# Rotary embedding on one core: half-size loads on two queues, earlier late loads, two more rows added by TensorE

## Chip, cores and metric

One core of a Trainium2 chip runs the kernel. The metric is the device time of one execution in microseconds (us); smaller is better. The time of a kernel is the median of its runs. "Profile" means one further execution, taken by the hardware profiler, whose span runs from the first instruction of the kernel to the last; its trace also has a record of every packet that the core's 16 DMA engines moved (queue, start, length, bytes).

## What is computed

`x` is 16 x 512 x 1024 in float32, 8192 vectors of 16 heads with 64 numbers each; `cos` and `sin` are 512 x 32. Each head is rotated:

```
x = x.reshape(batch, seq, num_heads, head_dim)
x1, x2 = x[..., :half_dim], x[..., half_dim:]
cos, sin = cos[None, :, None, :], sin[None, :, None, :]
rotated = concatenate([x1 * cos - x2 * sin, x1 * sin + x2 * cos], axis=-1)
```

So 33.5 MB are read and 33.5 MB written, with two multiplications and one addition for each number.

## The kernel before

**Tiles and rows.** The 8192 vectors are cut into eight tiles of 1024 (`TILES`, L33). A tile lies as 8 vectors on each of 128 partitions, and the kernel works by "rows": row `u` = 0 to 63 is one vector on each partition, 128 x 1024 numbers, and tile `t` has rows 8t to 8t + 7. A tile of 8 rows is 4 MB, with 32 KB on each partition. `x_sb` is a ring with places for 40 rows, five tiles; the sixth, seventh and eighth tile take the places of the first, second and third, and results are written over the input in the ring before they are stored.

**An entry of `TILES`** has the number of rows, the place in the ring, the pieces it is loaded in, the pieces it is stored in, and (last) the numbers of the stores that must have landed before it is loaded. Loads and stores are numbered in order of tiles. Before, the first tile is loaded as two halves (loads 0 and 1), all others whole (loads 2 to 8). The stores are 0 and 1 (halves of the first tile), 2 to 7 (whole tiles), 8 and 9 (halves of the last).

**Who does what for a row.** VectorE multiplies the row with the cosines (`mul`, L341) into one of three PSUM places (`NT1`). GpSimd multiplies the row, with its halves swapped, with the signed sines into one of six SBUF places `t2_sb` (`NT2`), for two rows at once (L308) or one (L165); VectorE does that itself for one row of each tile and a few more of the first (`V2`). The two products are added either by VectorE (`comb`, L350), or, where `PE2[u]` is set (L68), by TensorE, which multiplies `t2_sb` with the identity onto the PSUM place in four pieces of the row's two PSUM banks (L268), after which ScalarE copies the sum to `x_sb` (L230). Before, TensorE has rows 5 and 7 and, from row 8 to row 51, the second, fourth and sixth row of each tile. VectorE's order is written out: `mul(u)`, then `comb(u - 1)` where TensorE has not taken it (L357 to L365).

**The queues.** ScalarE's queue (`on_scalar`, L206) issues all loads of `x`: the six of the first five tiles at the very start, the other three ("late") behind a row of its copies (`BEHIND`, L45), after a wait for the stores that free their place. SyncE's queue (`on_sync`, L194) issues the two small tables of sines and cosines, and then every store, each as soon as its last row has been added. A queue hands its DMAs on in the order in which it issues them. The page calls ScalarE's queue q10 and SyncE's q1. Both feed the same 16 DMA engines, and each DMA of `x` is 8 packets on every engine: a packet is one partition's part, 32 KB for a whole tile, 16 KB for a half.

**Waiting for a load.** `wait_landed` (L190) makes GpSimd and VectorE wait at the first row of each load.

Of the kernel before, what the change touches and what calls it, by code (L numbers as in the profile page):

```python
# [6 lines left out]
def bass_split_heads_rope_kernel(  # L7
# [14 lines left out]
    R1 = seq // P  # L22
# [6 lines left out]
    COPY = mybir.ActivationFunctionType.Copy  # L29

    TILES = (  # L33
        (8, 0, (4, 4), (4, 4), ()),
        (8, 8, (8,), (8,), ()),
        (8, 16, (8,), (8,), ()),
        (8, 24, (8,), (8,), ()),
        (8, 32, (8,), (8,), ()),
        (8, 0, (8,), (8,), (0, 1)),
        (8, 8, (8,), (8,), (2,)),  # L40
        (8, 16, (8,), (4, 4), (3,)),
    )
    RING = 40

    BEHIND = {6: 21, 7: 28, 8: 37}  # L45
    first_row = [sum(t[0] for t in TILES[:i]) for i in range(len(TILES))]
    NU = sum(t[0] for t in TILES)
    assert NU * P == batch * seq
    NT = len(TILES)
# [2 lines left out]

    loads = []
    stores = []
    for t, (n, place, ins, outs, _) in enumerate(TILES):
        assert sum(ins) == n == sum(outs) and place + n <= RING
        loads += [(t, sum(ins[:i]), m) for i, m in enumerate(ins)]
        stores += [(t, sum(outs[:i]), m) for i, m in enumerate(outs)]
    load_at = {(t, o): i for i, (t, o, _) in enumerate(loads)}
    store_after = {first_row[t] + o + m - 1: i for i, (t, o, m) in enumerate(stores)}  # L60
    late = [i for i, (t, _, _) in enumerate(loads) if TILES[t][4]]
    awaited = sorted({k for t in TILES for k in t[4]})


    V_ROWS = {8: (3, 6)}
    V2 = [r in V_ROWS[TILES[t][0]] and (t == 0 or r != 6) for t, r in rows]

    PE2 = [u in (5, 7) or R1 * 2 <= u < NU - 3 * R1 and u % 8 in (1, 3, 5) for u in range(NU)]  # L68

    def count(flags):  # L70
        return [sum(flags[: u + 1]) for u in range(NU)]
# [5 lines left out]
    CUT = 5 * H // 8  # L77
    n_pe = count(PE2)
    n_comb = count([not a for a in PE2])

# [10 lines left out]
    with ExitStack() as stack:  # L91
# [13 lines left out]
        sem_in = [stack.enter_context(nc.semaphore(f"in{i}")) for i in range(len(loads))]  # L105
        sem_out = {k: stack.enter_context(nc.semaphore(f"out{k}")) for k in awaited}
# [24 lines left out]
        for n in SIZES:  # L131
            m = len(V_ROWS[n]) * HD
# [10 lines left out]
        xf = x.rearrange("b s d -> (b s) d")  # L143
        of = out.rearrange("b s h d -> (b s) (h d)")

        def in_dram(flat, t, o, m):
            n = TILES[t][0]
            run = flat[first_row[t] * P:(first_row[t] + n) * P, :].rearrange("(p r) d -> p (r d)", r=n)
            return run[:, o * dim:(o + m) * dim]

        def place_of(u):
            t, r = rows[u]
            return TILES[t][1] + r

        def in_sbuf(t, o, m):
            k = TILES[t][1] + o
            return x_sb[:, k:k + m].rearrange("p n h t d -> p (n h t d)")
# [14 lines left out]
        def wait_added(eng, u):  # L172
            if n_pe[u]:
                eng.wait_ge(sem_a, n_pe[u])
            if n_comb[u]:
                eng.wait_ge(sem_v, n_comb[u])

        def wait_t2_free(eng, u):
            if u >= NT2:
                v = u - NT2  # L180
                if PE2[v]:
                    eng.wait_ge(sem_e, n_pe[v])
                else:
                    eng.wait_ge(sem_v, n_comb[v])

        def load(eng, i):
            t, o, m = loads[i]
            eng.dma_start(in_sbuf(t, o, m), in_dram(xf, t, o, m)).then_inc(sem_in[i], 16)

        def wait_landed(eng, t, r):  # L190
            if (t, r) in load_at:
                eng.wait_ge(sem_in[load_at[t, r]], 16)

        def on_sync(sp):  # L194
            for c, table, sem in ((1, sin, sem_sin), (0, cos, sem_cos)):
                sp.dma_start(stage[:, c, :], table.rearrange("(s r) d -> s (r d)", r=R1)).then_inc(sem, 16)  # L196
            for u in range(NU):
                if u not in store_after:
                    continue
                k = store_after[u]  # L200
                t, o, m = stores[k]
                wait_added(sp, u)
                sp.dma_start(in_dram(of, t, o, m), in_sbuf(t, o, m)).then_inc(sem_out.get(k, sem_rest), 16)
            sp.wait_ge(sem_rest, 16 * (len(stores) - len(awaited)))

        def on_scalar(ae):  # L206
            early = [i for i in range(len(loads)) if i not in late]
            for i in early:
                load(ae, i)
            ae.wait_ge(sem_i, 2)  # L210
            for n in SIZES:
                m = n // R1
                ae.activation(  # L213
                    pick[n][:],
                    ident[:].rearrange("q (s k) -> q k s", k=m)[:, :, None, :].broadcast_to([P, m, m, P // m]),
                    COPY,
                ).then_inc(sem_g, 1)
            for i, n in enumerate(SIZES):
                ae.wait_ge(sem_t, i + 1)
                ae.activation(s_sb[n][:, :, 0, :], raw_sin[n], COPY, scale=-1.0)  # L220
                ae.activation(s_sb[n][:, :, 1, :], raw_sin[n], COPY).then_inc(sem_s, 1)  # L221
            for n in SIZES:
                v = V_ROWS[n]
                some = raw_sin[n][:, v[0]:v[-1] + 1:max(1, v[-1] - v[0]), :]
                ae.activation(v_ps[n][:, :, 0, :], some, COPY, scale=-1.0)
                ae.activation(v_ps[n][:, :, 1, :], some, COPY).then_inc(sem_s, 1)
            for u in range(NU):
                if PE2[u]:
                    ae.wait_ge(sem_e, n_pe[u])
                    ae.activation(xs[:, place_of(u), :], t1_ps[:, u % NT1, :], COPY).then_inc(sem_a, 1)  # L230
                for i in late:
                    if BEHIND[i] == u:
                        for j in TILES[loads[i][0]][4]:
                            ae.wait_ge(sem_out[j], 16)
                        load(ae, i)

        def on_tensor(pe):
            pe.wait_ge(sem_z, 1)
            for k in range(NT1):
                for b in range(EH):  # L240
                    pe.matmul(  # L241
                        t1_ps[:, k, b * BANK:(b + 1) * BANK], zero[:, 0:P], zero[:], start=True, stop=True
                    ).then_inc(sem_w, 1)
            pe.wait_ge(sem_g, len(SIZES))
            pe.wait_ge(sem_cos, 16)
            pe.wait_ge(sem_sin, 16)
            pe.wait_ge(sem_w, NT1 * EH)
            for n in SIZES:
                for c, to in enumerate((c_ps[n], raw_sin[n])):
                    for k in range(n // R1):  # L250
                        ins = pe.matmul(  # L251
                            to[:, k * R1:(k + 1) * R1, :].rearrange("p r d -> p (r d)"),
                            pick[n][:, k].rearrange("q b s -> q (b s)"),
                            stage[:, c, :],
                            start=c == 0,
                            stop=True,
                            skip_group_check=c == 1,
                        )
                ins.then_inc(sem_t, 1)
            for u in range(NU):  # L260
                if not PE2[u]:
                    continue
                if TWO[u - 1]:
                    pe.wait_ge(sem_q[(u - 1) % NT2], made[u - 1])
                pe.wait_ge(sem_q[u % NT2], made[u])
                t2 = t2_sb[:, u % NT2, :, :, :].rearrange("p h t d -> p (h t d)")
                for b in range(EH):
                    ins = pe.matmul(  # L268
                        t1_ps[:, u % NT1, b * BANK:(b + 1) * BANK],
                        ident[:],  # L270
                        t2[:, b * BANK:(b + 1) * BANK],
                        start=False,
                        stop=True,
                        skip_group_check=True,
                    )
                ins.then_inc(sem_e, 1)

        def on_gpsimd(pl):
# [12 lines left out]
            for u in range(NU):  # L291
# [9 lines left out]
                for v in range(u, u + m):  # L301
                    if v == u + m - 1 or PE2[v - NT2] != PE2[v + 1 - NT2]:
                        wait_t2_free(pl, v)
# [13 lines left out]
        def on_vector(ve):  # L317
# [39 lines left out]
            for u in range(NU + LEAD):  # L357
# [6 lines left out]
                if u >= LEAD and not ahead and not PE2[u - LEAD]:  # L364
                    comb(u - LEAD)  # L365

        on_sync(nc.sync)
        on_scalar(nc.scalar)
        on_gpsimd(nc.gpsimd)
        on_tensor(nc.tensor)  # L370
        on_vector(nc.vector)

# [32 lines left out]
```

## Time and profile before

| what | value |
|---|---|
| time, median of 3 runs | 161.31 us (161.09 to 161.41) |
| time of the profiled execution | 160.98 us |
| its span | 159.7 us |
| VectorE busy | 133.8 us (84%), 119 instructions |
| GpSimd busy | 126.3 us (79%), 40 instructions |
| TensorE busy | 60.5 us (38%), 90 matmuls |
| ScalarE busy | 22.1 us (14%), 25 instructions |
| moved by DMA | 67.25 MB, mean 421 GB/s over the span |
| ScalarE's queue, SyncE's queue | 49.4% and 49.1% of the time of 16 engines |

"Busy" is the sum of an engine's instructions. The page also cuts the span in 40 slices of 4 us and gives for each the busy share of every engine and of the DMA engines, as digits in tenths. "Landing" is the moment at which a DMA's completion has been counted by all 16 engines; until then no one may use its data.

### The profile page before, as it was taken

What the parts mean: (1) busy time and instruction counts of PE and PEld (TensorE: products, weight loads), DVE (VectorE), ACT (ScalarE), POOL (GpSimd) and SP (SyncE); (2) the same over time, 40 slices, a digit from 0 to 9 for tenths busy, and PEclk for the clock granted to TensorE, in tenths of its full rate; (3) what the DMA queues carried; (4) which work ended last, traced back from release to release, by engine and by line L of the source; (5) the groups of instructions that cost most, each with busy time, mean ns of one, the idle gap of its engine ahead of it and who ended that gap; (6) DMA issues with size and microseconds to landing.
All of it is one profiled execution on the core that took longest, in us unless ns stands there. A gap on an engine that the chain in (4) does not pass through costs nothing.

```text
span 159.7 us, 449 instructions
## 1 busy us (share of the span) xinstructions
PE 60.5 (38%) x90; PEld 20.9 (13%) x90; DVE 133.8 (84%) x119; ACT 22.1 (14%) x25; POOL 126.3 (79%) x40
## 2 busy tenths in 40 slices
PE   6013001893540954089509870854098100000000
PEld 1013001130110221023102220211022000000000
DVE  0005897999999999999899989999999899999600
ACT  0302000114220042011500250052002200000000
POOL 1003999999999999999999999999999699940000
PEclk9999999999996599755995576599755955555555
DMA  5999999999998999999999999999999999999896
GB/s 176 440 410 451 443 476 394 394 460 394 394 509 369 501 394 394 501 412 402 451 460 402 418 492 394 402 484 427 402 443 468 394 427 484 402 402 484 373 447 271
DMA packets 3025, 67.25 MB, mean 421 GB/s; under 512 B 336, under 2 KB 592, under 8 KB 592
## 3 DMA queue, kind: packets, MB, share of 16 engines
q10 hardware_dynamic: 1296, 33.56, 49.4%
q1 hardware_dynamic: 1728, 33.69, 49.1%
q14 instruction: 1, 0.01, 0.0%
HBM read 33.69 MB, written 33.55 MB: 421 GB/s over the span
## 4 chain that ended last, share of the span: by engine, by line
DVE 63%; PE 11%; POOL 8%; DMA 6%; ACT 3%; issue 2%; SPq 0%; POOLq 0%
DVE t_ps L341 35%; DVE x_sb L350 23%; PE t_ps L268 9%; DMA stage<-in_cos_dram 6%; DVE t_sb L165 6%; POOL t_sb L165 5%; POOL t_sb L308 3%; ACT x_sb L230 3%; PE tab_ps L251 1%; PE t_ps L251 1%; ACT sine L220 0%; SPq L196 0%; ACT sine L221 0%; POOLq L299 0%
## 5 line engine op out<-in xcount | busy, mean ns | idle before, releaser
L308 POOL TENSOR_TENSOR t_sb<-x_sb,sine 128x2048 f32<-128x2048 f32 x22 | 99.1, 4526 | 1.6 <-DMA x_sb<-in_x_dram 1.3
L341 DVE TENSOR_TENSOR t_ps<-x_sb,tab_ps 128x1024 f32<-128x1024 f32 x64 | 76.8, 1221 | 14.1 <-PE t_ps L251 12.5
L268 PE MATMUL t_ps<-t_sb,ident 128*128 128x512 f32 x76 | 55.7, 881 | 55.1 <-DVE t_ps L341 41.2
L350 DVE TENSOR_TENSOR x_sb<-t_ps,t_sb 128x1024 f32<-128x1024 f32 x45 | 54.5, 1215 | 1.6 <-POOL t_sb L308 0.9
L165 POOL TENSOR_TENSOR t_sb<-x_sb,sine 128x1024 f32<-128x1024 f32 (+1 forms) x12 | 27.3, 2288 | 13.0 <-ACT sine L221 13.0
L230 ACT ACTIVATE x_sb<-t_ps 128x1024 f32<-128x1024 f32 x19 | 19.5, 1024 | 91.5 <-PE t_ps L268 91.5
L268 PEld LDWEIGHTS t_ps<-t_sb,ident 128*128 128x128 f32 x76 | 18.4, 269 | 91.1 <-issue 59.6
L165 DVE TENSOR_TENSOR t_sb<-x_sb,tab_ps 128x1024 f32<-128x1024 f32 (+1 forms) x9 | 10.2, 1135 | 0.0
L251 PE MATMUL tab_ps<-stage,chosen 128*128 128x128 f32 x4 | 1.2, 454 | 7.5 <-DMA stage<-in_cos_dram 7.5
L241 PE MATMUL t_ps<-zero 128*128 128x512 bf16 x6 | 2.7, 627 | 1.2 <-DVE zero L318 1.2
L251 PEld LDWEIGHTS tab_ps<-stage,chosen 128*128 128x128 f32 x4 | 0.9, 322 | 8.4 <-issue 8.4
L213 ACT ACT_TABLE_LOAD x1 | 1.3, 1283 | 3.8 <-issue 3.8
L220 ACT ACTIVATE sine<-t_ps 128x256 f32<-128x256 f32 x1 | 0.4, 384 | 8.1 <-PE t_ps L251 8.1
L251 PE MATMUL t_ps<-stage,chosen 128*128 128x128 f32 x4 | 1.1, 421 | 0.0
L318 DVE MEMSET zero<- 128x256 uint32 x1 | 0.3, 272 | 0.9 <-PEq L387 0.9
L241 PEld LDWEIGHTS t_ps<-zero 128*128 128x128 bf16 x6 | 0.7, 135 | 2.4 <-DVE zero L318 1.2
L251 PEld LDWEIGHTS t_ps<-stage,chosen 128*128 128x128 f32 x4 | 1.0, 333 | 0.0
L279 POOL MEMSET ident<- 128x128 f32 x1 | 0.2, 205 | 0.3 <-POOLq L387 0.3
L213 ACT ACTIVATE chosen<-ident 128x256 f32<-128x256 f32 x1 | 0.4, 430 | 0.0
L221 ACT ACTIVATE sine<-t_ps 128x256 f32<-128x256 f32 x1 | 0.4, 377 | 0.0
L281 POOL TENSOR_SCALAR_AFFINE_SELECT ident<-ident 128x128 f32<-128x128 f32 x1 | 0.3, 293 | 0.1
L387 POOL MEMSET const-float32-0.0<- 128x1 f32 x1 | 0.1, 98 | 0.3 <-issue 0.3
(5 smaller groups left out, 0.7 us busy)
## 6 DMA issues: line engine op xcount, KB each, us to landing
x_sb<-in_x_dram ACTq DMA_DIRECT2D x7, 4096.0 KB, 29.1
out_dram<-x_sb SPq DMA_DIRECT2D x6, 4096.0 KB, 28.5
out_dram<-x_sb SPq DMA_DIRECT2D x4, 2048.0 KB, 15.4
x_sb<-in_x_dram ACTq DMA_DIRECT2D x2, 2048.0 KB, 9.7
stage<-in_sin_dram SPq DMA_DIRECT2D x1, 64.0 KB, 5.5
stage<-in_cos_dram SPq DMA_DIRECT2D x1, 64.0 KB, 10.2
```

The source lines that it names most:

```text
L165: return eng.tensor_tensor(t2_sb[:, u % NT2, a:b, :, :], swapped(place_of(u))[:, a:b], table[:, None, :, :].broadcast_to([P, b - a, 2, HALF]),
L213: ae.activation(pick[n][:], ident[:].rearrange("q (s k) -> q k s", k=m)[:, :, None, :].broadcast_to([P, m, m, P // m]), COPY,).then_inc(se ...
L220: ae.activation(s_sb[n][:, :, 0, :], raw_sin[n], COPY, scale=-1.0)
L221: ae.activation(s_sb[n][:, :, 1, :], raw_sin[n], COPY).then_inc(sem_s, 1)
L230: ae.activation(xs[:, place_of(u), :], t1_ps[:, u % NT1, :], COPY).then_inc(sem_a, 1)
L241: pe.matmul(t1_ps[:, k, b * BANK:(b + 1) * BANK], zero[:, 0:P], zero[:], start=True, stop=True).then_inc(sem_w, 1)
L251: ins = pe.matmul(to[:, k * R1:(k + 1) * R1, :].rearrange("p r d -> p (r d)"), pick[n][:, k].rearrange("q b s -> q (b s)"), stage[:, c, :] ...
L268: ins = pe.matmul(t1_ps[:, u % NT1, b * BANK:(b + 1) * BANK], ident[:], t2[:, b * BANK:(b + 1) * BANK], start=False, stop=True, skip_group ...
L281: pl.affine_select(out=ident[:], in_=ident[:], compare_op=mybir.AluOpType.is_equal, fill=0.0, base=0, pattern=[[-1, P]], channel_multiplier=1,
L308: pl.tensor_tensor(t2_sb[:, u % NT2:u % NT2 + 2].rearrange("p n h t d -> p (n h) t d"), x_sb[:, k:k + 2, :, ::-1, :].rearrange("p n h t d ...
L341: ve.tensor_tensor(t1_ps[:, u % NT1, :].rearrange("p (h d) -> p h d", d=HALF), x_sb[:, k, :, :, :].rearrange("p h t d -> p (h t) d"), c_ps ...
L350: ve.tensor_tensor(xs[:, place_of(u), :], t1_ps[:, u % NT1, :], t2_sb[:, u % NT2, :, :, :].rearrange("p h t d -> p (h t d)"), add,).then_i ...
```

## The change

- The second and third tile are loaded as two halves each. The first halves (loads 2 and 4) stay on ScalarE's queue; the second halves (loads 3 and 5) are issued by SyncE, behind the two tables and before all stores.
- The sixth tile is loaded as two halves too. With that the loads are numbered 0 to 11, and the late ones are 8 and 9 (halves of the sixth tile), 10 and 11 (the seventh and the eighth). They are issued behind rows 13, 21, 29 and 37, after a wait for store 0, 1, 2 and 3. Before, the three late loads stood behind rows 21, 28 and 37, the first of them after stores 0 and 1.
- Both halves of a tile other than the first count on one semaphore, and the tile's first row waits for both.
- `PE2` goes on to row 57: TensorE adds rows 53 and 57 as well.
- TensorE waits for the first load before it makes the tables.

```
     TILES = (
-        (8, 0, (4, 4), (4, 4), ()),
-        (8, 8, (8,), (8,), ()),
-        (8, 16, (8,), (8,), ()),
-        (8, 24, (8,), (8,), ()),
-        (8, 32, (8,), (8,), ()),
-        (8, 0, (8,), (8,), (0, 1)),
-        (8, 8, (8,), (8,), (2,)),
-        (8, 16, (8,), (4, 4), (3,)),
+        (8, 0, (4, 4), (4, 4)),
+        (8, 8, (4, 4), (8,)),
+        (8, 16, (4, 4), (8,)),
+        (8, 24, (8,), (8,)),
+        (8, 32, (8,), (8,)),
+        (8, 0, (4, 4), (8,)),
+        (8, 8, (8,), (8,)),
+        (8, 16, (8,), (4, 4)),
     )
...
-    BEHIND = {6: 21, 7: 28, 8: 37}
+    FREED_BY = {8: 0, 9: 1, 10: 2, 11: 3}
+    BEHIND = {8: 13, 9: 21, 10: 29, 11: 37}
+    ON_SYNC = (3, 5)
...
-    PE2 = [u in (5, 7) or R1 * 2 <= u < NU - 3 * R1 and u % 8 in (1, 3, 5) for u in range(NU)]
+    PE2 = [u in (5, 7) or R1 * 2 <= u < NU - 6 and u % 8 in (1, 3, 5) for u in range(NU)]
...
         def wait_landed(eng, t, r):
-            if (t, r) in load_at:
-                eng.wait_ge(sem_in[load_at[t, r]], 16)
+            if t == 0 and r == loads[1][1]:
+                eng.wait_ge(sem_in[1], 16)
+            if t > 0 and r == 0:
+                eng.wait_ge(sem_in[first_load[t]], 16 * len(TILES[t][2]))

         def on_sync(sp):
             for c, table, sem in ((1, sin, sem_sin), (0, cos, sem_cos)):
                 sp.dma_start(stage[:, c, :], table.rearrange("(s r) d -> s (r d)", r=R1)).then_inc(sem, 16)
+            for i in ON_SYNC:
+                load(sp, i)
...
-            early = [i for i in range(len(loads)) if i not in late]
+            early = [i for i in range(len(loads)) if i not in late and i not in ON_SYNC]
...
                 for i in late:
                     if BEHIND[i] == u:
-                        for j in TILES[loads[i][0]][4]:
-                            ae.wait_ge(sem_out[j], 16)
+                        ae.wait_ge(sem_out[FREED_BY[i]], 16)
                         load(ae, i)
...
             pe.wait_ge(sem_w, NT1 * EH)
+            pe.wait_ge(sem_in[0], 16)
```

More of the change, by code (lines that the diff above doesn't have):

```diff
@@ L54, in bass_split_heads_rope_kernel @@
     stores = []
-    for t, (n, place, ins, outs, _) in enumerate(TILES):
+    for t, (n, place, ins, outs) in enumerate(TILES):
         assert sum(ins) == n == sum(outs) and place + n <= RING
@@ L58, in bass_split_heads_rope_kernel @@
         stores += [(t, sum(outs[:i]), m) for i, m in enumerate(outs)]
-    load_at = {(t, o): i for i, (t, o, _) in enumerate(loads)}
     store_after = {first_row[t] + o + m - 1: i for i, (t, o, m) in enumerate(stores)}
-    late = [i for i, (t, _, _) in enumerate(loads) if TILES[t][4]]
-    awaited = sorted({k for t in TILES for k in t[4]})
+    first_load = [[v for v, _, _ in loads].index(t) for t in range(NT)]
+    late = sorted(FREED_BY)
+    awaited = sorted(FREED_BY.values())
     V_ROWS = {8: (3, 6)}
     V2 = [r in V_ROWS[TILES[t][0]] and (t == 0 or r != 6) for t, r in rows]
-    PE2 = [u in (5, 7) or R1 * 2 <= u < NU - 3 * R1 and u % 8 in (1, 3, 5) for u in range(NU)]
+    PE2 = [u in (5, 7) or R1 * 2 <= u < NU - 6 and u % 8 in (1, 3, 5) for u in range(NU)]
     def count(flags):
@@ L187, in load @@
             t, o, m = loads[i]
-            eng.dma_start(in_sbuf(t, o, m), in_dram(xf, t, o, m)).then_inc(sem_in[i], 16)
+            eng.dma_start(in_sbuf(t, o, m), in_dram(xf, t, o, m)).then_inc(sem_in[first_load[t] if t else i], 16)
         def wait_landed(eng, t, r):
-            if (t, r) in load_at:
-                eng.wait_ge(sem_in[load_at[t, r]], 16)
+            if t == 0 and r == loads[1][1]:
+                eng.wait_ge(sem_in[1], 16)
+            if t > 0 and r == 0:
+                eng.wait_ge(sem_in[first_load[t]], 16 * len(TILES[t][2]))
         def on_sync(sp):
```

## The prediction

> **What bounds the kernel now.** I read the page's slices and queues first, then the waits of SyncE's queue, then the end of the chain, then GpSimd's timeline and the DMA issues around the last load.
>
> ```profile
> DMA  5999999999998999999999999999999999999896
> ...
> q10 hardware_dynamic: 1296, 33.56, 49.4%
> q1 hardware_dynamic: 1728, 33.69, 49.1%
> ```
>
> The DMA engines are the bound: after the first slice they are busy to the end, and the two queues' packets take 98.5% of the span. In the trace's packet records, all 16 engines have a packet in flight from 2.2 us to 158.4. VectorE (84%) is idle mainly in the first 14 us and the last 9, and it does not set the end:
>
> ```profile
> SPq L204 <- DMA out_dram<-x_sb: 8.9, 1, 8.9
> ```
>
> SyncE's last act is to wait 8.9 us for stores. Store 9 was issued at 150.51; its first packet on a typical engine went at 153.7, since store 8 was still ahead of it, its last ended at 158.6 (159.36 on the slowest engine), landing at 159.70. An issue into an empty queue takes about 1.05 us to the first packet (loads and tables issued at 0.80: 1.80 and 1.89), so store 9 had some 2.1 us to spare on a typical engine. The chain shows what that store waited for:
>
> ```profile
> 147.04 1.14 DVE t_ps L341
> 148.18 2.25 DVE x_sb L350 x2
> ```
>
> VectorE's last additions end at 150.44, back to back since 126. What fed them is the last load:
>
> ```profile
> 125.86 4.52 POOL L308 TENSOR_TENSOR t_sb<-x_sb,sine 128x2048 f32<-128x2048 f32 x1 [1.28 <-DMA x_sb<-in_x_dram]
> 130.34 2.35 POOL L165 TENSOR_TENSOR t_sb<-x_sb,sine 128x1024 f32<-128x1024 f32 x1
> 132.64 8.99 POOL L308 TENSOR_TENSOR t_sb<-x_sb,sine 128x2048 f32<-128x2048 f32 x2
> ```
>
> GpSimd's rows 56 and 57 waited 1.28 us for the eighth tile, which landed at 125.80:
>
> ```profile
> x_sb<-in_x_dram ACTq DMA_DIRECT2D x1, 4096.0 KB, 29.1
> ```
>
> That is load 8 alone (a window from 90 us on): issued at 96.70, landed 29.1 us later. By its bytes alone it would need 8 packets of 1.21 us; the rest is queueing and sharing. So what counts is when the late tiles land, and how much store traffic goes ahead of them.
>
> **How the two queues share.** In the packet records each engine takes the queues in turn, one packet from each: at 5.5 us an engine has begun 5 of ScalarE's packets and 8 of SyncE's, at 10.0 it has begun 12 and 15. A packet of 512 bytes (27 ns), of 16 KB (0.61 us) and of 32 KB (1.21 us) each take one turn, and a DMA's completion (9 ns) takes one more: 9 turns a DMA, whatever its size. SyncE's queue is 3 turns ahead, from 2.5 us until it runs dry behind the tables at 11.0; it stays dry until store 0's first packet at 28.7. The Trainium skill ("DMA: Bandwidth & Descriptors", section "Queues, rings and completion order") also has the engines go round the queues, but in packets of typically 9 to 17 descriptors, which here would be a whole DMA's share of an engine; the records differ, with a change of queue after every single 32 KB. By that rule the eighth tile could land in the time that the first rival below gives.
>
> **The change, part by part.**
>
> *Three more DMAs.* Stores 7 and 8 landed 149.97 and 154.85, store 6 140.31: 9.66 us for 4 MB in 32 KB packets, 4.87 for 2 MB in 16 KB packets, so a tile in halves costs 2 x 4.87 - 9.66 = 0.08 us more. Three tiles: **+0.25 us** of DMA time, on the bound. The issues themselves (0.4 to 0.5 us each on ScalarE and SyncE, in the first 3 us) lie ahead of waits that end at 5 us and later.
>
> *Loads 3 and 5 on SyncE.* They go behind the tables and before store 0, which is issued at 24.2 and so stands behind load 5. The queue no longer runs dry from 11.0 to 28.7; the 3 turns of lead stay. Counting turns (16 KB against 16 KB: 9.73 us for 8 of each), load 3 ends at about 20, load 2 at 24, load 5 at 30, load 4 at 33. GpSimd wants tile 1 at 29.6 and tile 2 at 45.4: early enough. Store 0 then ends at about 42 (before, 41.3), store 1 at 57 (55.8). Fourth and fifth tile land at 50 and 65 (before 50.1 and 67.1) and are wanted at 61 and 77. So this half of the edit moves nothing that is waited for.
>
> *Late loads earlier.* Load 8 is issued behind row 13's copy (ends 46.9; store 0 has landed by 44), load 9 behind row 21 (62.7; store 1 by 59), load 10 behind row 29 (79.1; store 2 by 76), load 11 behind row 37 (95.8; store 3 by 91). ScalarE finds each wait already over. Were it not, its next copy (row 17 at 55.6, row 25 at 71.4, row 33 at 87.8) would be late, with 7 us or more of cover. But an earlier issue gains nothing: load 6 was issued at 61.8 and load 5's packets ended at 65.5, so ScalarE's queue was never empty before either.
>
> *The sixth tile in halves.* Here is the cost. The tile now needs 18 turns instead of 9, and SyncE's queue has by then 32 KB stores in each of its turns. Before, when load 8's last packet ended (123.5 on a typical engine), 80 turns of ScalarE's queue had gone, and of SyncE's stores 0 to 4 and 3 packets of store 5. After, the last packet of load 11 is turn 9 x 9 + 8 = 89 of its queue, and with the lead of 3 SyncE's is at turn 92: nine turns each for sine, cosine, loads 3 and 5, stores 0 to 5 make 90, and two more are packets of store 6. All loads have gone in both cases, so the difference is 5 + 2 = 7 store packets: 7 x 1.21 = 8.5 us, and 0.25 for the halves. The stores are there: store 5 is issued at 99.1 and its turn comes at 108, store 6 at about 117 and its turn comes at 128. The eighth tile lands at 125.8 + 8.7 = **134.5**. The same count at load 9 and load 10 also gives 7 packets: sixth tile 87.0 + 8.7 = 95.7, seventh 106.4 + 8.7 = 115.1.
>
> *Who is late then.* GpSimd wanted the sixth tile at 92.6 and VectorE at 96.7: GpSimd starts 3.1 us late, ends rows 40 and 41 at 100.3, and VectorE's addition of row 40, due at 100.1, loses 0.2. The seventh is wanted by GpSimd at 108.7 (111.6 by now) and by VectorE at 112.5; with 115.1, GpSimd's rows 48 and 49 end at 119.7 and VectorE's addition of row 48 comes at 119.7 instead of 115.9: 3.8 late. The eighth: GpSimd's rows 56 and 57 run from 134.6 to 139.1, and VectorE's addition of row 56, which stood at 133.4, at **139.1**.
>
> *Rows 53 and 57 to TensorE.* Each takes an addition of 1.13 us (pitch of L350 in the timeline) from VectorE and adds four matmuls and a copy (row 51: 3.8 and 1.0 us) to engines that were idle from 125.4. Row 53's gain only lets VectorE wait for the eighth tile earlier (it would be through by about 132.8). Row 57's counts: from the addition of row 56 to the issue of store 9 it was 150.51 - 133.39 = 17.1 us, now 16.0. Row 57's copy ends at 139.1 + 3.8 + 1.0 = 144.0, and row 60's multiplication, which needs its PSUM place, comes at about 144.7: covered by 0.7 us.
>
> *Sum.* Store 9 is issued at 139.1 + 16.0 = 155.1. Without a gap the engines would be through with store 8 at 153.6 + 0.25 = 153.9, so they run dry. First packet 156.15, eight packets of 0.61 to 161.05, landing 0.35 later: span **161.4**, against 159.7, +1.7 us. The profiled execution took 160.98, which would make 162.7; the median shown is 161.31, and with the same difference **163.0 us**. Stores 7 and 8 do not start a gap earlier: store 7 goes out when row 55 is added, 136.9, and is wanted at 139.5; store 8 at 147.2, wanted at 149.
>
> TensorE's new wait for load 0 (landed 8.2) is over before the one for the cosines (11.4) ends. The new waits for both halves cost what is counted above.
>
> One cost is not seen in the trace. When store 0 came in, 16 load packets from 27.2 on took 1.35 to 1.79 us instead of 1.21; with their neighbours this is 0.54 us of DMA time. Whether it returns when store 0 stands behind load 5 in the same queue is bounded by 0 and 0.54 us; I take that it returns, as it did where stores first met loads.
>
> **The rivals.**
>
> *The tiles land in time, not slower.* Span = landing of the eighth tile + 26.9, but not under 159.7 + 0.25. The price falls to nothing if the tile lands by 133.0, that is two packets earlier: if the lead of 3 turns is lost when load 3 follows the tables, or sharing goes by bytes. If shares went by bytes, ScalarE's 28 MB up to load 11 would meet 24 MB of SyncE's (the tables take the first 4 MB's turns): loads 3 and 5 with 4 MB, stores 0 to 5 with 20. Then 5 packets more instead of 7, landing 132.1. For it: the engines are never idle before, and total traffic is the same. Against: the constant lead in the records. Time: 161.31 + 0.25 = 161.55, within 0.2%. The skill's rule that it does not help to spread transfers over several issuing engines, as all run on the same 16 ("DMA: Bandwidth & Descriptors", section "Rules for kernel authors"), stands beside this rival; the trace agrees in so far as packets of both queues take 1.21 us each.
>
> *Faster.* The same, and the 0.54 us at store 0 do not return: 161.31 + 0.25 - 0.54 = 161.0, at the edge of 0.2%.
>
> *Worse.* Two packets more go ahead of each late tile (a store that keeps its turns while ScalarE's next load is being fetched): landing 136.9, and 165.4. For it: nothing but the fact that the tiles' delays have no cover left.
>
> **How the numbers follow.** Forecast 163.0, chance 0.58 (from 161.7 to 164.3, a packet either way); not slower 0.24; faster 0.06; worse 0.12. A measurement of this kernel can tell about 0.2% (0.32 us) from no change. Slower by more: 0.58 + 0.12 = 0.70; within: 0.24; faster: 0.06. The range from 161.1 to 165.4 takes in the forecast, most of the not-slower case and half of the worse one.
>
> **What would show it.** In the profile after: GpSimd's wait for `x_sb` grows from 1.3 us to about 3 + 3.5 + 3.5, at rows 40, 48 and 56; the eighth tile lands near 134.5; VectorE idles some 2 us each ahead of rows 48 and 56; the last wait of SyncE is 6.3 us instead of 8.9, and a DMA slice near the end falls below 9. Wrong if the sixth tile lands before 92.6, or if the last slices stay full with store 9 issued before 153.

## The result, and the profile after

The changed kernel takes **164.06 us** (median of 6 runs, 162.98 to 165.55) against 161.28 (161.09 to 161.41): ratio 1.0161, 95% interval 1.013 to 1.0192, slower. One slow run (165.55) is in the median and not in the ratio. The forecast was 163.0, slower, range 161.1 to 165.4. The profiled execution took 162.98 us with a span of 161.4, where the working gave 162.7 and 161.4. It is the shortest of the six: the other spans go from 161.8 to 163.5.

First the page of the changed kernel, the slices and queues:

```profile
DMA  5999999999999999999999999999999999999957
...
q1 hardware_dynamic: 2016, 37.88, 54.7%
q10 hardware_dynamic: 1440, 29.36, 43.0%
```

Before, the last slices were 8, 9, 6 and the two queues' shares added up to 98.5%; now there is a 5 ahead of the end and the sum is 97.7% of a longer span. The same bytes are moved with a hole in them. Three windows of the core place it (columns: PE, PEld, DVE, ACT and POOL busy, granted clock, DMA share, GB/s):

```profile
126.00:154.00 28.00, 6.18 (x10) 1.85 (x8) 24.67 (x23) 3.07 (x3) 20.83 (x6) 0.65 1.00 430
154.00:156.20 2.20, 0.00 (x0) 0.00 (x0) 1.06 (x1) 0.00 (x0) 0.00 (x0) 0.50 0.30 127
```

The DMA engines are full until 154.0, then at 30% for 2.2 us: store 9 is not there yet. SyncE's waits say the same from the other side, the last store takes 5.9 us after SyncE begins to wait for it, instead of 8.9, because nothing is ahead of it:

```profile
SPq L213 <- DMA out_dram<-x_sb: 5.9, 1, 5.9
```

The chain of the changed kernel shows what the store waited for (columns: start, length, what):

```profile
94.50 40.03 DMA x_sb<-in_x_dram
134.53 0.07 issue
134.59 4.52 POOL t_sb L317
139.11 0.03 issue
139.14 1.22 DVE x_sb L359
...
152.81 2.25 DVE x_sb L359 x2
```

Load 11 was issued at 94.50 and landed 40.0 us later, at 134.53, 11 us longer than the last load before; from there GpSimd's rows 56 and 57 and VectorE's additions run without a break to store 9's issue at 155.14. GpSimd's timeline has the same wait at each of the three late tiles:

```profile
95.90 4.51 POOL L317 TENSOR_TENSOR t_sb<-x_sb,sine 128x2048 f32<-128x2048 f32 x1 [2.97 <-DMA x_sb<-in_x_dram]
...
115.24 4.50 POOL L317 TENSOR_TENSOR t_sb<-x_sb,sine 128x2048 f32<-128x2048 f32 x1 [3.55 <-DMA x_sb<-in_x_dram]
...
134.59 4.51 POOL L317 TENSOR_TENSOR t_sb<-x_sb,sine 128x2048 f32<-128x2048 f32 x1 [3.56 <-DMA x_sb<-in_x_dram]
```

Why do the loads come late? A window from 78 to 96 us, in which the changed kernel loads the second half of the sixth tile, gives each queue's packets, MB and share of the engines. Before:

```profile
q10 hardware_dynamic: 143, 4.16, 53.6%
q1 hardware_dynamic: 128, 3.70, 47.7%
```

After:

```profile
q1 hardware_dynamic: 176, 5.24, 67.5%
q10 hardware_dynamic: 182, 2.56, 33.2%
```

The packet counts of the two queues are nearly equal in both kernels; the bytes are not. With 16 KB packets of loads against 32 KB packets of stores, ScalarE's queue gets a third of the engines.

### The profile page after: what moved, and what is told of

Read it like the earlier page. It is cut to its first block, busy times and chain, and to the rows that moved or that the text cites. A ratio compares the mean times of both kernels' runs of the same rounds, so it can differ in the third digit from the quotient of the medians.

```text
span 161.4 us, 469 instructions
## 1 busy us (share of the span) xinstructions
PE 62.6 (39%) x98; PEld 21.8 (13%) x98; DVE 131.8 (82%) x117; ACT 24.1 (15%) x27; POOL 126.3 (78%) x40
## 4 chain that ended last, share of the span: by engine, by line
DVE 44%; DMA 31%; POOL 11%; PE 7%; ACT 1%; issue 1%; SPq 0%
DMA x_sb<-in_x_dram 25%; DVE t_ps L350 24%; DVE x_sb L359 16%; DMA stage<-in_cos_dram 7%; PE t_ps L277 6%; POOL t_sb L317 6%; POOL t_sb L168 5%; DVE t_sb L168 4%; PE tab_ps L260 1%; ACT x_sb L239 1%; PE t_ps L260 1%; ACT sine L229 0%; SPq L203 0%; ACT sine L230 0%
## 5 line engine op out<-in xcount | busy, mean ns | idle before, releaser
L277 PE MATMUL t_ps<-t_sb,ident 128*128 128x512 f32 x84 | 57.8, 830 | 71.2 <-POOL t_sb L317 38.3
L359 DVE TENSOR_TENSOR x_sb<-t_ps,t_sb 128x1024 f32<-128x1024 f32 x43 | 52.1, 1216 | 4.2 <-POOL t_sb L317 3.5
L239 ACT ACTIVATE x_sb<-t_ps 128x1024 f32<-128x1024 f32 x21 | 21.5, 1024 | 107.7 <-PE t_ps L277 107.7
L277 PEld LDWEIGHTS t_ps<-t_sb,ident 128*128 128x128 f32 x84 | 19.2, 254 | 108.5 <-issue 50.0
```

The source lines that it names most:

```text
L277: ins = pe.matmul(t1_ps[:, u % NT1, b * BANK:(b + 1) * BANK], ident[:], t2[:, b * BANK:(b + 1) * BANK], start=False, stop=True, skip_group ...
L359: ve.tensor_tensor(xs[:, place_of(u), :], t1_ps[:, u % NT1, :], t2_sb[:, u % NT2, :, :, :].rearrange("p h t d -> p (h t d)"), add,).then_i ...
```

## The experiments

The rivals to turns by packets: the loads on SyncE hold the stores back; shares go by bytes; more DMAs cost by themselves. "Time outside the span" is the time of an execution less its span. The kernel before ran beside each group: medians 160.98 to 161.05 us, spans 159.7 to 159.8, time outside the span 1.24 to 1.27. In the edits `...` stands for lines left out; where a load waits for several stores, the loop over them is among these.

**1. The sixth tile whole again.**

```
-        (8, 0, (4, 4), (8,)),
+        (8, 0, (8,), (8,)),
...
-    FREED_BY = {8: 0, 9: 1, 10: 2, 11: 3}
-    BEHIND = {8: 13, 9: 21, 10: 29, 11: 37}
+    FREED_BY = {8: (0, 1), 9: (2,), 10: (3,)}
+    BEHIND = {8: 21, 9: 29, 10: 37}
```

> After, with the sixth tile loaded whole again (behind row 21, after stores 0 and 1); second and third tile still in halves on two queues, TensorE still adds rows 53 and 57. Theory (queues take turns packet by packet, so a DMA costs nine turns whatever its size): the last load is turn 80 of ScalarE's queue again, SyncE's is then at turn 83, which is packet 2 of store 5; before it was packet 3. The eighth tile lands about 124.8 us, GpSimd waits about 1 us for it or less, no DMA gap before store 9, span 159.9, time within 0.2% of the kernel before (about 161.5). Rival (the loads on SyncE, which hold store 0 back behind load 5, make the late tiles late): the eighth tile still lands near 134 and the time stays near 164.

Measured: 161.88 us, ratio 1.0053 (1.0041 to 1.0065). GpSimd and SyncE wait for their DMAs:

```profile
POOL t_sb L318 <- DMA x_sb<-in_x_dram: 0.3, 1, 0.3
```

```profile
SPq L213 <- DMA out_dram<-x_sb: 11.3, 1, 11.3
```

The eighth tile landed at 125.08, the spans are 159.8 to 160.2, and store 9 waits 11.3 us, in line behind store 8. The rival falls: loads 3 and 5 are still on SyncE. This kernel also issues the late loads behind rows 21, 29 and 37 again; that the earlier rows of the change are not the cause is shown by 4 and 12, which keep them. The time is 0.4 us over what was expected, all of it outside the span (1.8 us; see 5 to 8).

**2. Second and third tile whole again (the first two lines), the sixth in halves.**

```
-        (8, 8, (4, 4), (8,)),
-        (8, 16, (4, 4), (8,)),
+        (8, 8, (8,), (8,)),
+        (8, 16, (8,), (8,)),
...
-    FREED_BY = {8: 0, 9: 1, 10: 2, 11: 3}
-    BEHIND = {8: 13, 9: 21, 10: 29, 11: 37}
-    ON_SYNC = (3, 5)
+    FREED_BY = {6: 0, 7: 1, 8: 2, 9: 3}
+    BEHIND = {6: 13, 7: 21, 8: 29, 9: 37}
+    ON_SYNC = ()
```

> After, with second and third tile loaded whole on ScalarE's queue again; only the sixth is in halves, behind rows 13 and 21, and TensorE adds rows 53 and 57. Theory (turns): the last load is turn 89 of ScalarE's queue, SyncE's is at turn 75, packet 3 of store 6: eight store packets more than before, the eighth tile lands at 135.6, span 162.5, one packet (1.2 us) later than after. Time about 165 (1.1 us over after). Rival (loads on SyncE are the cause): tiles land as before, 125.8, time about 161.4.

Measured: 165.65 us, ratio 1.0296 (1.0283 to 1.031), profiled span 163.5. GpSimd's timeline at the three late tiles:

```profile
96.86 4.51 POOL L317 TENSOR_TENSOR t_sb<-x_sb,sine 128x2048 f32<-128x2048 f32 x1 [4.10 <-DMA x_sb<-in_x_dram]
...
117.33 4.51 POOL L317 TENSOR_TENSOR t_sb<-x_sb,sine 128x2048 f32<-128x2048 f32 x1 [4.68 <-DMA x_sb<-in_x_dram]
...
136.69 4.51 POOL L317 TENSOR_TENSOR t_sb<-x_sb,sine 128x2048 f32<-128x2048 f32 x1 [3.56 <-DMA x_sb<-in_x_dram]
```

The sixth tile came at 96.8, 1.0 us later than after, where one packet (1.2) was counted. The other two came 1.0 us later than counted: a packet at 96.44 took 2.00 us instead of 1.21, another at 109.51 took 1.36, both on the same engine by the order of its packets, and a landing waits for the slowest engine. The halves of the sixth tile make the whole loss without the early halves; those, on SyncE, give one packet back.

**3. TensorE without rows 53 and 57.**

```
-    PE2 = [u in (5, 7) or R1 * 2 <= u < NU - 6 and u % 8 in (1, 3, 5) for u in range(NU)]
+    PE2 = [u in (5, 7) or R1 * 2 <= u < NU - 3 * R1 and u % 8 in (1, 3, 5) for u in range(NU)]
```

> After, with VectorE adding rows 53 and 57 as before; all loads as in after. Theory: landings as in after (95.8, 115.2, 134.5); the addition of row 53 falls into VectorE's wait for the eighth tile and costs nothing, that of row 57 comes after it and costs 1.13 us, store 9 is issued about 156.3, span 162.5, time 1.1 us over after (about 165.2). Rival (TensorE's rows cost what they save, by row 60's wait for its PSUM place): time as after or below it, 164.0 or less.

Measured: 165.15 us, ratio 1.0259 (1.023 to 1.0289), profiled span 163.0. VectorE at row 56, here and (second fence) in the changed kernel:

```profile
134.97 1.23 DVE L350 TENSOR_TENSOR t_ps<-x_sb,tab_ps 128x1024 f32<-128x1024 f32 x1 [0.64 <-DMA x_sb<-in_x_dram]
```

```profile
134.55 1.23 DVE L350 TENSOR_TENSOR t_ps<-x_sb,tab_ps 128x1024 f32<-128x1024 f32 x1 [2.23 <-DMA x_sb<-in_x_dram]
```

Row 53's addition went into VectorE's wait for the eighth tile, which shrank from 2.23 to 0.64 us, and cost nothing; row 57's comes after it. From the tile's landing to the issue of store 9 it is 21.74 us here (134.95 to 156.69) and 20.61 in the changed kernel (134.53 to 155.14): 1.13. The landing itself is 0.42 us later than in the changed kernel's first trace, where one packet at 107.48 took 1.71 us. This part of the change helps the changed kernel's span by 1.13; in experiment 5, where the DMA engines set the end, it is worth nothing in the span. That the time itself met the expected 165.2 is partly luck: the median span (163.65) is some 1.4 us over the changed kernel's, and the time outside it, 1.5 us, is shorter by 0.3 to 0.5 (see 5 to 8).

**4. The stores of the second to fifth tile in halves too.**

```
-        (8, 8, (4, 4), (8,)),
-        (8, 16, (4, 4), (8,)),
-        (8, 24, (8,), (8,)),
-        (8, 32, (8,), (8,)),
+        (8, 8, (4, 4), (4, 4)),
+        (8, 16, (4, 4), (4, 4)),
+        (8, 24, (8,), (4, 4)),
+        (8, 32, (8,), (4, 4)),
...
-    FREED_BY = {8: 0, 9: 1, 10: 2, 11: 3}
+    FREED_BY = {8: (0,), 9: (1,), 10: (2, 3), 11: (4, 5)}
```

> After, with the stores of the second to fifth tile in halves too (16 KB packets), the late loads waiting for the halves that free their place. Theory (turns): SyncE's turns now move half the bytes, so the loads get their share back: sixth tile landed near 85 us, eighth near 121, no DMA gap, span 159.7 + 0.25 + 4 x 0.08 = 160.3, time about 161.9, 2 us under after. Rival (shares go by bytes, or the halves themselves slow the engines): the tiles land no earlier than in after, or the time stays at 164 or more.

Measured: 162.01 us, ratio 1.0061 (1.0049 to 1.0073), span 160.1. The window from 78 to 96 us:

```profile
q10 hardware_dynamic: 193, 4.74, 61.0%
q1 hardware_dynamic: 221, 3.10, 40.2%
```

The sixth tile landed at 84.4, the eighth at 121.0. Halving more transfers took 2 us off: halves are harmless against halves. This is against shares by bytes and against a price of the halves as such.

**5 to 8. What is outside the span, and where the runs differ.** Kernel 5 is before with `NU - 6` in `PE2` (the edit of 3, reversed) and nothing else; kernel 6 is experiment 1 with before's `PE2`; kernel 7 is before with three semaphores that nothing uses; kernel 8 is the changed kernel again.

> Before, with only one part of the change: TensorE adds rows 53 and 57 too; all loads as before. Theory: the DMA engines set the end, so the span stays at 159.7, with store 9 issued some 2 us earlier. What is open is the time outside the span: it was 1.25 us in the runs of before, 1.5 in the experiment without these two rows, and 1.6 to 2.1 in the kernels with them. If TensorE's and ScalarE's longer programs cause part of it, the time rises by 0.3 to 0.6 us over before with an unchanged span; if the loads alone cause it, the time equals before within 0.1 us.

> Before's late loads and before's TensorE rows, with one part of the change: second and third tile in halves, loads 3 and 5 on SyncE. Theory: eighth tile lands near 125.0, span 159.9 (0.16 us for two more tiles in 16 KB packets). Time outside the span: about 1.5 us if it goes with the loads, about 1.25 if it goes with TensorE's rows; so the time is 161.4 or 161.15.

> Before, with three semaphores more that nothing uses (the changed kernel declares three more). Theory: nothing changes, 161.0 us. Rival: part of the time outside the span goes with the number of semaphores, and the time rises by 0.1 us or more with the span unchanged.

> The changed kernel, unaltered, for a second trace and beside the others on one chip. Its spans so far went from 161.4 to 163.5 us, where those of before stay at 159.7 to 159.8. Theory: the end now hangs on three landings in a row, each of which waits for the slowest of 16 engines, so single slow packets ahead of them pass through to the end; a trace with a longer span shows the seventh or eighth tile landing later than 115.2 and 134.5 by as much, and the same 20.6 us from that landing to the issue of store 9. Rival: the compute after the landing takes longer than 20.6 us (TensorE's granted clock), or the DMA engines are slower throughout.

| kernel | time, us | ratio (interval) | median span | outside the span |
|---|---|---|---|---|
| 5, TensorE's rows only | 161.71 | 1.0037 (1.0023 to 1.0051) | 159.8 | 1.93 |
| 6, early halves only | 161.35 | 1.0018 (1.001 to 1.0027) | 159.8 | 1.52 |
| 7, three semaphores | 161.04 | 0.9994 (0.9986 to 1.0003) | 159.8 | 1.26 |
| 8, changed kernel again | 164.24 | 1.0201 (1.0177 to 1.0225) | 162.3 | 1.81 |

TensorE's rows cost 0.67 us and the early halves 0.26 us where no span shows them; the semaphores cost nothing. The two do not add up: the changed kernel, which has both, is 0.55 us over before there, and its single executions lie at 1.5 to 1.6 or at 1.8 to 2.05. The profiled run of kernel 8 had a span of 163.3, 1.9 us over the first trace of the same program:

```profile
97.11 4.51 POOL L317 TENSOR_TENSOR t_sb<-x_sb,sine 128x2048 f32<-128x2048 f32 x1 [4.98 <-DMA x_sb<-in_x_dram]
...
117.07 4.51 POOL L317 TENSOR_TENSOR t_sb<-x_sb,sine 128x2048 f32<-128x2048 f32 x1 [4.17 <-DMA x_sb<-in_x_dram]
...
136.46 4.51 POOL L317 TENSOR_TENSOR t_sb<-x_sb,sine 128x2048 f32<-128x2048 f32 x1 [3.59 <-DMA x_sb<-in_x_dram]
```

The eighth tile landed at 136.39, 1.86 later, and store 9 went out 20.61 us after that, as in the first trace. In the packet records the lead of SyncE's queue is 4 turns at 9 us here, 3 in the first trace: one 32 KB packet more ahead of every late tile, 1.21 us, which is the delay of the sixth tile. The other 0.63 us is one packet on one engine at 106.36 that took 1.84 us. So the later landing passes to the end as expected, and the rival (slower compute, slower engines throughout) falls; but two thirds of the delay are the lead, which the expectation did not have. With before's late loads the same has no way to the end: kernel 7 has a lead of 4 as well, its eighth tile landed at 126.81, 1.0 us after before's, and its span is 159.8.

**9 to 11. Each row or a step?** Kernel 9 is before with row 51 given to VectorE (`u < 50`), 10 with row 53 alone given to TensorE (`u < 54`), 11 with eight more matmuls of zeros at TensorE's start.

> Before, with row 51 added by VectorE instead of TensorE. Store 9 is issued about 1.1 us later (151.6), still ahead of the end of store 8's packets (153.6), so the span stays at 159.7 to 159.8. If the time outside the span goes with the rows that TensorE adds (0.67 us for two), it falls from 1.26 to about 0.9 and the time to 160.7; if it goes in steps of the program's length, it stays at 1.26 and the time at 161.0.

> Before, with row 53 alone added by TensorE too (not row 57). Span 159.7 to 159.8. Time outside the span 1.26 + 0.34 = 1.6 us and the time 161.4 if it goes with each row; 1.26 or 1.93 if it goes in steps.

> Before, with eight more matmuls of zeros on TensorE at the start, where it waits for the tables (they are done by about 9 us, the tables land at 11.4); ScalarE's and VectorE's programs are unchanged. Span 159.7 to 159.8. Time outside the span about 1.9 us (time 161.7) if it is the length of TensorE's program that costs; 1.26 (time 161.0) if it is ScalarE's two more copies or something else of these rows.

Measured: 161.08 (ratio 0.9996 to 1.0014), 161.01 (0.9991 to 1.0009) and 161.78 us (1.0035 to 1.0062); spans 159.8, 159.8 and 159.7, time outside the span 1.26, 1.26 and 2.08. It is a step: one row more or less changes nothing, two rows or eight matmuls cost about 0.7 us, and ScalarE's copies are not needed for it. In kernel 5's trace, whose span ends at 160.1, the queues' packets in a window from 159 to 163 us:

```profile
q1 hardware_dynamic: 4, 0.02, 1.0%
q14 instruction: 1, 0.01, 0.7%
```

and in kernel 11's:

```profile
q8 instruction: 1, 0.02, 1.6%
q1 hardware_dynamic: 1, 0.00, 0.0%
```

An instruction packet (8 KB at 161.9, 16 KB at 161.1) comes after the last instruction of the span; the trace of before has none there. All 14 traces sort the same way. Six have such a packet (1, 2, 4, 5, 11 and 12, all with 98 matmuls), and these executions took 1.8 to 2.1 us outside the span. The other eight have none and took 1.2 to 1.6 us, among them both profiled executions of the changed kernel (1.58 and 1.54), which lie at the lower of its two values. So the packet and the longer time go together, execution by execution. That a longer TensorE program makes the core fetch one more block at the end fits this and the step, but it is not shown: no run tells whose instructions the packet holds, and the 0.26 us of the early halves have no packet to go with.

**12. One useless DMA more.**

```
+        spare = stack.enter_context(nc.sbuf_tensor([P, R1 * HALF], fp32))
...
+            sp.dma_start(spare[:], sin.rearrange("(s r) d -> s (r d)", r=R1)).then_inc(sem_rest, 16)
             for i in ON_SYNC:
                 load(sp, i)
...
```

> After, with one useless DMA more: SyncE loads the table of sines a second time, into a spare tile that nobody reads, between the two tables and load 3. Theory (turns): the 64 KB take nine turns, some 0.3 us of DMA time, and push loads 3 and 5 and every store nine turns back against ScalarE's loads. When load 11 ends, SyncE's queue is at packet 2 of store 5 instead of packet 2 of store 6, nine 32 KB turns with eight packets and a completion less (9.7 us): the eighth tile lands near 125, there is no gap before store 9, the span is 160.0 to 160.3 and the time about 162.0, some 2 us under after. Rival (more DMAs and a longer queue on SyncE are what costs): the time is that of after, 164.2, or more.

Measured: 162.35 us, ratio 1.0093 (1.0071 to 1.0115) to before; 1.9 us under the 164.24 that the changed kernel took in another group. GpSimd at the eighth tile, and SyncE's last wait:

```profile
125.23 4.52 POOL L319 TENSOR_TENSOR t_sb<-x_sb,sine 128x2048 f32<-128x2048 f32 x1 [0.67 <-DMA x_sb<-in_x_dram]
```

```profile
SPq L215 <- DMA out_dram<-x_sb: 11.7, 1, 11.7
```

The eighth tile landed at 125.16, 9.4 us earlier, because 64 KB were moved for nothing on the other queue. Nine turns were expected to be worth 9.7 us. By none of the rivals named above would one more DMA make the kernel faster.

No version here beats the kernel before: those without a gap ahead of store 9 have median spans of 159.7 to 160.3, and the DMA engines are busy throughout. Two of the six executions of 12 had spans of 161.0 and 161.4; no trace shows why.

## Why the prediction was right, and where it was short

- *The bound.* Right: each kernel whose late tiles come in time (1, 4 to 7, 9 to 12) has a span of 159.6 to 160.3 in its profile. Store 8's packets ended at 153.93 at the earliest in the changed kernel and store 9's first went at 155.97, where 153.9 and 156.15 were counted.
- *Nine turns a DMA, a lead of 3, seven store packets more.* Right to the packet. Landings of the sixth, seventh and eighth tile: forecast 95.7, 115.1, 134.5; measured 95.83, 115.17, 134.53. When the last load's last data packet ended on a typical engine (123.47 before, 132.40 after), that engine had moved 27 and 34 packets of 32 KB of stores, seven more; the same count gives 26 in 1, 35 in 2, 26 in 12 and 35 in kernel 8, each as the turns have it. "A packet either way" was also right: the lead differs from start to start, 3 or 4 turns in the traces.
- *Early halves on SyncE move nothing that is waited for.* Right for what waits. They were one packet of help (2), which the counting had and the text did not say.
- *Three more DMAs, +0.25.* Not settled. Experiment 6, with two of the three, has a median span within 0.1 us of before, where 0.16 was expected; the term is of the size of the reading.
- *First store's slow packets.* They returned, again just ahead of the store's own first packet (31.6): 16 KB packets that began around 29 to 31 us took up to 1.28 us, with their neighbours about 0.7 us of DMA time (0.54 before).
- *Who is late then.* Right: waits of 2.97, 3.55 and 3.56 us at GpSimd (3.1, 3.5, 3.5), store 9 at 155.14 (155.1), a gap ahead of it. SyncE's last wait, forecast at 6.3 and measured at 5.9, is the same time counted from two starts: the working counts from the issue of store 9, the profile from the end of that issue.
- *TensorE's rows.* Right inside the span: 1.13 us for row 57 and nothing for row 53 (3). Row 60's multiplication did not wait.
- *Where it was short.* The last step of the sum, "with the same difference 163.0 us", carried the difference of two spans over to the medians. That supposes that the time outside the span stays, and that the counted span is the usual one. The time outside the span rose from 1.26 to some 1.8 to 2.0 us in the medians (by TensorE's longer program and a little by the loads), and the median span of the changed kernel is 162.1 to 162.3 rather than 161.4. In the two traces lead and slow packets differ; the other executions have no trace. Beside kernel 8, where the spans of both kernels are on record, the span grew by 2.5 us and the time outside it by 0.55, and the medians lie 3.2 us apart. In the first group they lie 2.8 apart, as the kernel before took 161.28 there and 160.98 to 161.05 in all later groups.
- *Luck.* That the profiled span met 161.4 to the digit is partly luck: of the changed kernel's eleven executions it is the shortest, and the others go from 161.8 to 163.5.

The Trainium skill ("DMA: Bandwidth & Descriptors", section "Rules for kernel authors") says that spreading DMAs over issuing engines gives no bandwidth, as all run on the same 16. The runs agree on the bandwidth: 6 moves two loads to SyncE at the same span. But which queue a DMA stands in, and what it meets there, decided when it landed: 12 moved the eighth tile by 9.4 us with 64 KB. The Trainium skill ("DMA: Bandwidth & Descriptors", section "Queues, rings and completion order") has packets of typically 9 to 17 descriptors; here one row of 16 or 32 KB was a packet.

## What to carry to other kernels

In these traces two full queues share the engines by packets, so the queue with the smaller packets gets fewer bytes: halving a load that runs against whole stores doubles its turns, and the 4 MB of the sixth tile took 29.1 us from its first packet to the next load's instead of 19.4. Before splitting a transfer, count the turns of its queue and what the other queue moves in them, up to the last transfer that anyone waits for; a kernel that DMA bounds, as this one, has no slack to lose there but the wait of its last store.

## What the runs showed that was not expected

- Time outside the span is a cost of its own: with before's loads it is 1.26 us for TensorE's 86, 90 and 94 matmuls and 1.9 to 2.1 for 98, with equal spans.
- The start of the two queues is not always the same: at 9 us SyncE's lead was 3 turns in twelve of the 14 traces and 4 in the other two (7 and 8). Where loads on SyncE keep both queues full, it lasts to the late tiles.
- A landing waits for the slowest of 16 engines: single packets of 1.7 to 2.0 us on one engine moved the eighth tile's landing by 0.4 to 1.0 us in 2, 3 and 8, where the late tiles are on the path.
